# One product of 512 columns instead of two of 256 in the RWKV projections and both output projections of a two-layer trunk

## The chip, the cores and the metric

One NeuronCore of a Trainium2 chip runs the whole program; there is no other core and no collective. The metric is device time of one execution in microseconds (us). The engines are TensorE (PE, matmuls; PEld are its weight loads), VectorE (DVE), ScalarE (ACT), GpSimd (POOL) and SyncE (SP, which issues most transfers). All accumulate or read in float32; the large products are done in the reduced form that the profile shows as fp32r.

## The reference

Two layers over a sequence of 256 tokens of width 2048, each a token mixer and an MLP of width 8192 with a squared ReLU, all modulated by a conditioning vector `c`:

```
mod = c_act @ ada_w[i] + ada_b[i]
hmix = rms_norm(x) * (1 + sc1) + sh1
y = dsa_mixer(hmix, ...)        # layer 0: indexer, top-k, attention, then  out @ w_o
y = rwkv7_mixer(hmix, ...)      # layer 1
x = x + g1 * y
hff = rms_norm(x) * (1 + sc2) + sh2
x = x + g2 * (jnp.square(jax.nn.relu(hff @ mlp_w1[i])) @ mlp_w2[i])
```

Inside the second mixer stand four square products of 2048 by 2048: `r = xr @ w_r`, `k = xk @ w_k`, `v = xv @ w_v`, and at the end `(o * g) @ w_o`. Between them runs a scan over the tokens with a state per head. A last RMS norm closes the program.

## The kernel before, in words

Activations lie transposed: 16 tiles `x[f]` of 128 features by 256 tokens. To keep float32 accuracy with fp32r products, every operand is split into a high part (rounded to fp32r by a cast on ACT) and a low part (the rest, a subtraction on DVE or POOL). A moving tile holds both, side by side, as 128 x 512: columns 0 to 255 high, 256 to 511 low. A weight piece of 128 x 512 becomes two tiles, `whi` (L92) and `wlo` (L94). `acc3` (L178 to L186) multiplies one weight block of 128 x 128 with one moving tile in three matmuls of 256 columns, which all add into the same 256 columns of a PSUM bank: high weights by high part (L184), high weights by low part (L185), low weights by high part (L186). I call these three a term. `dense` takes a bank and runs `acc3` over all terms of one output tile; one call has 16 terms in the projections `b_w_r`, `b_w_k`, `b_w_v`, and 1 to 4 in the output projections.

Who reads the bank: for r, k and v one ACT copy (L735, L863, L899). For an output projection (`out_group`, L402 to L409) one DVE operation, `x[f] = p * gate + x[f]` (L409). The output projection of layer 0 (`a_w_o`) has 48 calls of four terms that run beside the attention heads, and then 16 of three terms and 16 of one term at its end, with L409 reading. The one of layer 1 (`b_w_o`) has 48 calls of four terms and 32 of two terms, of which the last 16 come after the last head of the scan. Counted in terms that is 256 for each of the five: `a_w_o`, r, k, v, `b_w_o`, 1,280 in all.

A PSUM tile takes a whole bank, whatever its width. Kind "d" has two banks, kind "m" two, and "a", "b", "i", "j" one each. `s.kinds` says which kinds `dense` goes through: "d" alone in the heads, for k, for v and in the scan, "dm" for r, and "dcm" at the end of layer 0's output projection and in the MLPs ("c" is "a" and "b" in turn).

The order on each engine is not written out: a scheduler builds it from priorities and its own simulation, and each engine then runs its list strictly in order. So every queue has a fixed order, and a late instruction holds up all behind it. The MLP that follows each mixer begins on DVE, ACT and POOL with its input tiles `h` (L355, L356), which need the finished `x[f]`; each product of the MLP adds over all 16 of them. `ada_block` (L224) puts long products on DVE, in between, for the modulation of later layers.

Of the kernel before, what the change touches and what calls it, by code (L numbers as in the profile page):

```python
# [12 lines left out]
OP = mybir.AluOpType  # L13
# [3 lines left out]
P = 128  # L17
D = 2048
S = 256
# [82 lines left out]
class Trunk:  # L102
# [76 lines left out]
    def acc3(s, out, terms):  # L179
        mm = s.nc.tensor.matmul  # L180
        n = len(terms)
        for i, (wh, wl, m) in enumerate(terms):
            w = m.shape[-1] // 2
            mm(out, wh, m[:, :w], start=i == 0, stop=False)  # L184
            mm(out, wh, m[:, w:], start=False, stop=False)  # L185
            mm(out, wl, m[:, :w], start=False, stop=i == n - 1)  # L186

    def dense(s, w, movs, cols):
        s.turn += 1
# [213 lines left out]
    def out_group(s, name, layer, block, g, movs, first=0):  # L403

        w = s.wload(s.io[name][block * 4 + g, :, first * 512:(first + len(movs)) * 512])
        for o in range(4):
            f = g * 4 + o
            p = s.dense(w, movs, [k * 512 + o * P for k in range(len(movs))])
            s.nc.vector.scalar_tensor_tensor(s.x[f], p, s.m(layer, 2, f), s.x[f], op0=OP.mult, op1=OP.add)  # L409


    def angles(s, freq, which):
# [277 lines left out]
    def rwkv_project(s, keep):  # L690
        nc, io = s.nc, s.io
        mm = nc.tensor.matmul
# [27 lines left out]
        cols = [k * P for k in range(16)]  # L720

        xm = []
        for i in range(NF + LAG):
            if i < NF:
                normed(i)
            if i >= LAG:
                k = i - LAG
# [2 lines left out]
        s.xv = []  # L730
        for f in range(NF):
            w = s.wload(io["b_w_r"][f])
            p = s.dense(w, xm, cols)
            t = s.B()
            nc.scalar.copy(t, p)  # L735
            nc.sync.dma_start(s.rd[f], t)
            wl1 = s.wload(io["b_lora1"][f // 4][:, f % 4 * 448:f % 4 * 448 + 448], "l")
            d = delta(f)
# [2 lines left out]
            for p, m, c in ((hid[0], xw, 0), (hid[1], xa, 96), (hid[2], xg, 192), (hid[3], xg, 320)):  # L741
                wh, wl = wl1.at(c)
# [20 lines left out]
        for f in range(NF + 1):  # L763
            if f < NF:
                w = s.wload(io["b_w_k"][f])
                pk = s.dense(w, xm, cols)
            if f:
                s.elements(f - 1, pp, omka, wa0)
            if f == NF:
                s.vs[0] = s.value(0, keep.tile([P, S], F32, name="v0"))  # L770
            pp = pk
# [52 lines left out]
    def elements(s, f, pk, omka, wa0):  # L824
# [35 lines left out]
        nc.gpsimd.tensor_copy(s.pc[:, f, :].unsqueeze(2), pp[:, :, 64:65])  # L860

        k, kk, sq = s.B(), s.B(), s.B()
        nc.scalar.copy(k, pk)  # L863
        nc.vector.tensor_scalar(kk, k, s.v("k_k", f), None, op0=OP.mult)
        nc.scalar.activation(sq, kk, AF.Square)
        ap = s.B()
# [29 lines left out]

    def value(s, f, v):
        w = s.wload(s.io["b_w_v"][f])
        s.nc.scalar.copy(v, s.dense(w, s.xv, [i * P for i in range(16)]))  # L899
        return v  # L900

    def prepare(s, f):
# [350 lines left out]
```

## Time and profile before

| | |
|---|---|
| median of 3 runs | 2779.71 us (2779.48 to 2797.15) |
| profiled execution | 2790.62 us, span 2788.7 us |
| PE busy | 94% of the span, 24,884 matmuls |
| PE weight loads | 88% |
| DVE busy | 70% |
| ACT, POOL busy | 47%, 48% |
| mean granted TensorE clock | 0.963 of full speed |

The stages, by the first and last instruction of their lines in the trace: layer 0's mixer up to 247 us, its attention heads 247 to 426 us, the end of its output projection from there to about 467 us, overlapping with the first MLP (to 1243 us); r from 1282 to 1390 us, k from 1390 to 1546 us, v and the scan from 1546 to 2010 us, the last output projections to 2040 us, the second MLP to the end. Matmuls are pipelined: the profile gives each a duration of about 0.28 us although the next starts 0.12 us later, so the step from start to start is what a matmul costs, and "busy" is not the same as used to the full. The profiled execution is 0.4% longer than the median of the runs.

### The profile page before, as it was taken

The numbers are of one execution on the slowest core, as the hardware profiler recorded it, in microseconds if no ns is written. First come the engines' busy times: TensorE is split into PE (matmuls) and PEld (weight loads), VectorE is DVE, ScalarE is ACT, GpSimd is POOL, SyncE is SP. The second block draws the span as 40 slices with busy tenths as digits, with TensorE's granted clock in tenths as the row PEclk, the third lists the DMA queues.
The fourth block names the chain that finished last, engine by engine and source line by source line (L and its number), as shares of the span: only waits on it lengthen the run. The fifth ranks groups of instructions, "written<-read, shape, count | busy, mean of one in ns | idle before, by whom it ended". The sixth has DMA issues, their size and how long they took to land. (4 is left out here: it accounts for less than half of the span.)

```text
span 2788.7 us, 64443 instructions
## 1 busy us (share of the span) xinstructions
PE 2630.8 (94%) x24884; PEld 2446.9 (88%) x24884; DVE 1957.3 (70%) x3183; ACT 1309.4 (47%) x2852; POOL 1345.3 (48%) x1121
## 2 busy tenths in 40 slices
PE   6898998999999999988889999999899999999998
PEld 4566778999999999888888888888799999999998
DVE  2266568998999999968787655666688377473553
ACT  3334435445444444446555343444455455454553
POOL 1243327566577576655655411233465445444444
PEclk9899999999999999999999887999999999999999
DMA  9997745889899898855557522343467767555553
GB/s 370 393 339 270 255 135 187 312 308 348 283 338 328 286 347 311 302 167 152 172 181 246 173 83 75 89 117 97 146 225 219 222 213 243 183 182 184 182 183 115
DMA packets 263620, 624.73 MB, mean 224 GB/s; under 512 B 29328, under 2 KB 43024, under 8 KB 238352
## 3 DMA queue, kind: packets, MB, share of 16 engines
q1 hardware_dynamic: 256400, 608.03, 65.2%
q10 hardware_dynamic: 6912, 12.59, 1.2%
q8 instruction: 195, 3.19, 0.5%
q14 instruction: 113, 0.93, 0.1%
HBM read 603.72 MB, written 16.78 MB: 222 GB/s over the span
## 5 line engine op out<-in xcount | busy, mean ns | idle before, releaser
L94 POOL TENSOR_TENSOR wlo<-raw,whi 128x512 fp32r<-128x512 f32 x364 | 587.1, 1622 | 544.5 <-ACT whi L92 417.2
L92 ACT CAST whi<-raw 128x512 fp32r<-128x512 f32 x856 | 513.0, 619 | 404.7 <-PE ps_d L185 149.1
L94 DVE TENSOR_TENSOR wlo<-raw,whi 128x512 fp32r<-128x512 f32 x492 | 436.5, 892 | 222.6 <-ACT whi L92 211.0
L94 POOL TENSOR_TENSOR wlo<-more,whi 128x512 fp32r<-128x512 f32 x181 | 263.7, 1460 | 322.7 <-ACT whi L92 165.6
L224 DVE CUSTOM_DVE_ANT_0 araw<-araw,cb 128x2048 f32<-128x2048 f32 x124 | 342.6, 2776 | 4.6 <-DMA araw<-ada_w_in 4.6
L184 PE MATMUL ps_d<-A,whi 128*128 128x256 f32 x1058 | 309.4, 293 | 10.6 <-ACT B L863 6.2
L92 ACT CAST whi<-more 128x512 fp32r<-128x512 f32 x366 | 222.0, 618 | 199.0 <-PE ps_d L185 48.5
L185 PE MATMUL ps_d<-A,whi 128*128 128x256 f32 x1058 | 303.5, 287 | 2.3 <-DVE A L198 2.2
L186 PE MATMUL ps_d<-A,wlo 128*128 128x256 f32 x1058 | 303.1, 287 | 0.5 <-DVE wlo L94 0.5
L94 DVE TENSOR_TENSOR wlo<-more,whi 128x512 fp32r<-128x512 f32 (+1 forms) x185 | 174.3, 943 | 138.8 <-ACT whi L92 135.6
L184 PEld LDWEIGHTS ps_d<-A,whi 128*128 128x128 f32 x1058 | 205.4, 195 | 26.2 <-ACT B L863 7.2
L185 PEld LDWEIGHTS ps_d<-A,whi 128*128 128x128 f32 x1058 | 205.5, 194 | 4.8 <-DVE A L198 3.8
L186 PEld LDWEIGHTS ps_d<-A,wlo 128*128 128x128 f32 x1058 | 205.5, 194 | 1.5 <-DVE wlo L94 0.7
L375 ACT ACTIVATE B<-B,sm 128x256 f32<-128x256 f32 x128 | 65.3, 510 | 247.5 <-DVE B L374 247.4
L185 PE MATMUL ps_d<-h,whi 128*128 128x258 f32 x552 | 157.5, 285 | 3.7 <-DVE h L356 3.7
L186 PE MATMUL ps_d<-h,wlo 128*128 128x258 f32 x552 | 155.8, 282 | 2.5 <-DVE wlo L94 2.4
L184 PE MATMUL ps_d<-h,whi 128*128 128x258 f32 x552 | 156.7, 284 | 0.0
L184 PE MATMUL ps_m<-h,whi 128*128 128x258 f32 x540 | 153.4, 284 | 0.0
L185 PE MATMUL ps_m<-h,whi 128*128 128x258 f32 x540 | 153.1, 284 | 0.0
L186 PE MATMUL ps_m<-h,wlo 128*128 128x258 f32 x540 | 152.1, 282 | 0.0
L376 DVE TENSOR_TENSOR B<-B 128x256 f32<-128x256 f32 x128 | 111.5, 871 | 52.9 <-ACT B L375 52.9
L184 PE MATMUL ps_m<-A,whi 128*128 128x256 f32 x506 | 145.1, 287 | 1.1 <-ACT whi L92 1.1
(552 smaller groups left out, 8773.8 us busy)
## 6 DMA issues: line engine op xcount, KB each, us to landing
araw<-ada_w_in SPq DMA_DIRECT2D x192, 1024.0 KB, 7.2
raw<-mlp_w_in SPq DMA_DIRECT2D x614, 256.0 KB, 4.6
more<-mlp_w_in SPq DMA_DIRECT2D x410, 256.0 KB, 4.1
raw<-b_w_r_in SPq DMA_DIRECT2D x64, 256.0 KB, 3.6
raw<-b_w_k_in SPq DMA_DIRECT2D x64, 256.0 KB, 3.8
raw<-b_w_v_in SPq DMA_DIRECT2D x64, 256.0 KB, 3.6
raw<-b_w_o_in SPq DMA_DIRECT2D x64, 256.0 KB, 3.5
hd<-A ACTq DMA_DIRECT2D x48, 256.0 KB, 4.3
```

The costliest lines, as they stand in the source:

```text
L92: t.nc.scalar.copy(hi[:, :n], r)
L94: e.tensor_tensor(lo[:, :n], r, hi[:, :n].bitcast(F32), op=OP.subtract)
L184: mm(out, wh, m[:, :w], start=i == 0, stop=False)
L185: mm(out, wh, m[:, w:], start=False, stop=False)
L186: mm(out, wl, m[:, :w], start=False, stop=i == n - 1)
L224: nc.vector.tensor_tensor_reduce(out=w, in0=w, in1=s.cb, scale=1.0, scalar=0.0, op0=OP.mult, op1=OP.add, accum_out=acc[:, k:k + 1])
L375: nc.scalar.activation(r, u, AF.Relu, bias=c)
L376: nc.vector.tensor_tensor(q, r, r, op=OP.mult)
```

## The change

`wide` replaces `dense` in the five places. It gives the whole moving tile (512 columns, high and low) to one matmul with the high weights, so that columns 0 to 255 of the bank collect high by high and columns 256 to 511 high by low; the low weights still meet the high part alone, into columns 0 to 255. A term is then one matmul of 512 columns and one of 256. The two halves of the bank are added afterwards: for r, k and v by `join`, an ACT copy of the right half to a new tile of 256 columns from the ring `B`, then a DVE addition of the left half and that copy; in `out_group` by running the DVE operation twice, once for each half.

```diff
+    def wide(s, w, movs, cols, kind=None):
+        mm = s.nc.tensor.matmul
+        s.turn += 1
+        p = s.bank(kind or s.kinds[s.turn % len(s.kinds)])
+        n = len(movs)
+        for i, (c, m) in enumerate(zip(cols, movs)):
+            wh, wl = w.at(c)
+            if i:
+                mm(p[:, :S], wl, m[:, :S], start=False, stop=False)
+                mm(p, wh, m, start=False, stop=i == n - 1)
+            else:
+                mm(p, wh, m, start=True, stop=False)
+                mm(p[:, :S], wl, m[:, :S], start=False, stop=n == 1)
+        return p
+
+    def join(s, out, p):
+        t = s.B()
+        s.nc.scalar.copy(t, p[:, S:])
+        s.nc.vector.tensor_tensor(out, p[:, :S], t, op=OP.add)
...
-            p = s.dense(w, movs, [k * 512 + o * P for k in range(len(movs))])
-            s.nc.vector.scalar_tensor_tensor(s.x[f], p, s.m(layer, 2, f), s.x[f], op0=OP.mult, op1=OP.add)
+            p = s.wide(w, movs, [k * 512 + o * P for k in range(len(movs))])
+            for k in range(2):
+                s.nc.vector.scalar_tensor_tensor(s.x[f], p[:, k * S:(k + 1) * S], s.m(layer, 2, f), s.x[f],
+                                                 op0=OP.mult, op1=OP.add)
...
-            p = s.dense(w, xm, cols)
+            p = s.wide(w, xm, cols)
             t = s.B()
-            nc.scalar.copy(t, p)
+            s.join(t, p)
...
-                pk = s.dense(w, xm, cols)
+                pk = s.wide(w, xm, cols)
...
-        nc.scalar.copy(k, pk)
+        s.join(k, pk)
...
-        s.nc.scalar.copy(v, s.dense(w, s.xv, [i * P for i in range(16)]))
+        s.join(v, s.wide(w, s.xv, [i * P for i in range(16)]))
```

The scheduler makes a new order of it. Three places, of which the first is on PE, in the last products of r (bank kinds "d" and "m"; `xm` tiles are named `A`, the last four `o`). Before:

```order
L184 MATMUL ps_m<-o,whi 128x256
L185 MATMUL ps_m<-o,whi 128x256
L186 MATMUL ps_m<-o,wlo 128x256
L184 MATMUL ps_m<-o,whi 128x256
L185 MATMUL ps_m<-o,whi 128x256
L186 MATMUL ps_m<-o,wlo 128x256
```

and with the change, where L198 and L199 are the two matmuls of `wide`:

```order
L198 MATMUL ps_d<-A,wlo 128x256
L199 MATMUL ps_d<-A,whi 128x512
L198 MATMUL ps_d<-A,wlo 128x256
L199 MATMUL ps_d<-A,whi 128x512
L198 MATMUL ps_d<-A,wlo 128x256
```

Three rows of a term have become two, one of them 512 wide.

The second is DVE at the seam between layer 0's output projection and the first MLP, where the one-term products are read (L409) and the MLP's first input tiles `h` (L356) are made. Before:

```order
L409 SCALAR_TENSOR_TENSOR x_68<-ps_b,mod_84,x_68 128x256
L409 SCALAR_TENSOR_TENSOR x_69<-ps_m,mod_84,x_69 128x256
L356 SCALAR_TENSOR_TENSOR h<-x_66,mod_84,h 128x256
L409 SCALAR_TENSOR_TENSOR x_70<-ps_d,mod_84,x_70 128x256
L409 SCALAR_TENSOR_TENSOR x_71<-ps_a,mod_84,x_71 128x256
L409 SCALAR_TENSOR_TENSOR x_72<-ps_m,mod_84,x_72 128x256
L94 TENSOR_TENSOR wlo<-raw,whi 128x512
L409 SCALAR_TENSOR_TENSOR x_73<-ps_d,mod_84,x_73 128x256
L356 SCALAR_TENSOR_TENSOR h<-x_67,mod_84,h 128x256
```

and with the change (L409 is now L433, L356 is L379):

```order
L379 SCALAR_TENSOR_TENSOR h<-x_66,mod_84,h 128x256
L433 SCALAR_TENSOR_TENSOR x_72<-ps_m,mod_84,x_72 128x256
L94 TENSOR_TENSOR xlo<-more,xhi 128x512
L433 SCALAR_TENSOR_TENSOR x_73<-ps_d,mod_84,x_73 128x256
L379 SCALAR_TENSOR_TENSOR h<-x_67,mod_84,h 128x256
L433 SCALAR_TENSOR_TENSOR x_70<-ps_d,mod_84,x_70 128x256
L433 SCALAR_TENSOR_TENSOR x_71<-ps_a,mod_84,x_71 128x256
L379 SCALAR_TENSOR_TENSOR h<-x_68,mod_84,h 128x256
L433 SCALAR_TENSOR_TENSOR x_74<-ps_b,mod_84,x_74 128x256
L379 SCALAR_TENSOR_TENSOR h<-x_69,mod_84,h 128x256
L433 SCALAR_TENSOR_TENSOR x_72<-ps_m,mod_84,x_72 128x256
```

Each `x` tile has two readings of a bank now, and the scheduler puts other work between the two. From the last copy of an attention output (L666) to the first result of the MLP (L374) DVE has 39 such readings before and 86 with the change: the 32 calls of the end and seven earlier ones before, the 32 and eleven now. The rest of the list is the same but for one weight piece more.

The third is DVE in k, where before the bank was read by ACT alone and no row of DVE stood for it. With the change (L209 is the addition of `join`, L889 the next use of k, L879 and L918 belong to the same stage):

```order
L879 SCALAR_TENSOR_TENSOR B<-cst,B 128x256
L209 TENSOR_TENSOR B<-ps_d,B 128x256
L889 TENSOR_SCALAR B<-B,vec 128x256
L94 TENSOR_TENSOR llo<-raw,lhi 128x512
L894 TENSOR_SCALAR B<-B,vec,omka 128x256
L895 TENSOR_TENSOR B<-B 128x256
L879 SCALAR_TENSOR_TENSOR B<-cst,B 128x256
L918 SCALAR_TENSOR_TENSOR A<-B,vec 128x256
L94 TENSOR_TENSOR wlo<-raw,whi 128x512
L209 TENSOR_TENSOR B<-ps_d,B 128x256
```

The bank is free for the next product only after that addition, which stands in DVE's list behind work of other kinds.

## Rows read from the trace of the kernel before

**Rows 1.** The page: span, busy time and share of each engine, count.

```profile
span 2788.7 us, 64443 instructions
PE 2630.8 (94%) x24884; PEld 2446.9 (88%) x24884; DVE 1957.3 (70%) x3183; ACT 1309.4 (47%) x2852; POOL 1345.3 (48%) x1121
```

**Rows 2.** Windows of stages: length, busy us of each engine, clock, DMA share.

```profile
core 0: us, PE busy (x) PEld busy (x) DVE busy (x) ACT busy (x) POOL busy (x), PEclk, DMA share, GB/s
...
247.00:426.00 179.00, 166.74 (x1113) 127.02 (x1112) 105.07 (x260) 68.79 (x177) 47.89 (x40) 0.95 0.58 201
...
1282.00:1390.00 108.00, 96.76 (x762) 94.63 (x761) 85.92 (x158) 63.33 (x147) 63.64 (x48) 0.95 0.63 182
1390.00:1546.00 156.00, 141.31 (x1123) 132.96 (x1124) 126.08 (x239) 89.16 (x206) 92.26 (x162) 0.97 0.66 206
...
1617.00:2010.00 393.00, 383.50 (x6673) 329.13 (x6671) 257.27 (x714) 161.76 (x440) 107.11 (x96) 0.94 0.33 95
```

**Rows 3.** Windows of both seams, columns as in rows 2.

```profile
426.00:444.00 18.00, 18.00 (x152) 18.00 (x152) 9.17 (x18) 7.63 (x15) 9.14 (x7) 1.00 0.47 143
444.00:476.00 32.00, 26.65 (x192) 24.85 (x192) 31.66 (x51) 23.74 (x51) 28.96 (x53) 0.95 0.75 252
...
2013.00:2046.00 33.00, 28.07 (x185) 26.84 (x185) 29.21 (x42) 23.47 (x50) 29.06 (x48) 0.82 0.60 190
```

**Rows 4.** Waits of PE from 444 to 492 us: total, times, longest.

```profile
PE ps_d L185 <- DVE h L356: 3.7, 5, 1.6
PE ps_a L185 <- DVE h L356: 2.9, 1, 2.9
```

**Rows 5.** Timeline of PE, 256 columns: start, duration, line, form; 32 steps apart.

```profile
427.15 0.28 PE L184 MATMUL ps_d<-A,whi 128*128 128x256 f32 x1
...
430.99 0.28 PE L186 MATMUL ps_d<-A,wlo 128*128 128x256 f32 x1
```

**Rows 6.** Timeline of PE, 512 columns: 19 steps, then four in another stretch.

```profile
231.59 0.40 PE L591 MATMUL ps_d<-wlo,A 128*128 128x512 f32 x1
...
235.90 0.39 PE L592 MATMUL ps_d<-whi,A 128*128 128x512 f32 x1
...
207.30 0.40 PE L591 MATMUL ps_d<-wlo,A 128*128 128x512 f32 x1
...
208.23 0.40 PE L592 MATMUL ps_d<-whi,A 128*128 128x512 f32 x1
```

**Rows 7.** Groups by line on DVE, heads, scan, and an addition from PSUM.

```profile
L409 DVE SCALAR_TENSOR_TENSOR x<-ps_d,mod,x 128x256 f32<-128x256 f32 x41 | 19.7, 479 | 20.3 <-PE ps_d L186 20.2
...
L94 DVE TENSOR_TENSOR wlo<-raw,whi 128x512 fp32r<-128x512 f32 x63 | 52.7, 841 | 24.6 <-ACT whi L92 21.9 <-PE ps_d L186 1.7 <-PE ps_d L185 0.5
L409 DVE SCALAR_TENSOR_TENSOR x<-ps_d,mod,x 128x256 f32<-128x256 f32 x80 | 38.3, 480 | 20.2 <-PE ps_d L186 19.1
...
L446 DVE TENSOR_TENSOR B<-ps_m,B 128x256 f32<-128x256 f32 x16 | 6.7, 417 | 7.7 <-PE ps_m L444 6.6 <-POOL wlo L94 1.1
```

**Rows 8.** Timeline of DVE at both seams: readings, waits in brackets.

```profile
434.55 0.48 DVE L409 SCALAR_TENSOR_TENSOR x<-ps_d,mod,x 128x256 f32<-128x256 f32 x1 [2.38 <-PE ps_d L186]
...
444.98 0.47 DVE L409 SCALAR_TENSOR_TENSOR x<-ps_m,mod,x 128x256 f32<-128x256 f32 x1
445.37 0.47 DVE L409 SCALAR_TENSOR_TENSOR x<-ps_d,mod,x 128x256 f32<-128x256 f32 x1
...
471.24 4.44 DVE L356 SCALAR_TENSOR_TENSOR h<-x,mod,h 128x256 fp32r<-128x256 f32 x5
...
2046.83 0.16 DVE L266 TENSOR_SCALAR sm<-ps_m 128x2 f32<-128x2 f32 x1 [1.35 <-PE ps_m L306]
```

**Rows 9.** Waits of PE in k, 1390 to 1546 us.

```profile
PE ps_d L184 <- ACT B L863: 6.2, 5, 2.2
```

**Rows 10.** Timeline of PE: a first matmul after a wait, and the next.

```profile
457.25 0.38 PE L184 MATMUL ps_d<-o,whi 128*128 128x256 f32 x1 [0.78 <-DVE x L409]
457.47 0.28 PE L185 MATMUL ps_d<-o,whi 128*128 128x256 f32 x1
```

## Prediction

> **What bounds the kernel now.** I read the page first: PE is busy for 94% of the span, DVE for 70%, ACT and POOL under half [rows 1]. By stages PE is nearly full in all that the change touches: 166.7 of 179 us in the attention heads, 96.8 of 108 in r, 141.3 of 156 in k, 383.5 of 393 in the scan [rows 2]. So PE sets the pace, and time that PE's matmuls give back counts, as long as nobody makes PE wait instead. Two stages differ. At the seam between layer 0's output projection and the first MLP, DVE is busy for 31.66 of 32 us while PE has 26.65 [rows 3], and PE waits there for the tiles `h` that DVE makes, 3.7 and 2.9 us [rows 4]: DVE sets the pace. At the seam after the scan it is 29.21 of 33 us on DVE against 28.07 on PE, at a granted clock of 0.82, a mixture of the two levels [rows 3].
>
> **What the change gives on PE.** It removes 1,280 matmuls of 256 columns, one for each term, and makes 1,280 others twice as wide; the columns streamed stay the same. What it gives is the part of a matmul that doesn't grow with its width. The steps show it. 32 steps of 256 columns take 430.99 - 427.15 = 3.84 us, 0.1200 us each [rows 5]. 19 steps of 512 columns, which layer 0's value projection already has, take 235.90 - 231.59 = 4.31 us, 0.2268 us each [rows 6]. Two narrow ones cost 0.2400 us, one wide one 0.2268: 0.0132 us saved, and 1,280 x 0.0132 = 16.9 us. Another stretch of four wide steps takes 0.93 us, 0.2325 each [rows 6]; by that it would be 0.0075 and 9.6 us. I take 16.9, since the longer stretch has the most steps in a row, and keep 9.6 as the other end.
>
> The Trainium skill speaks against this size: "TensorE: Matmul & The Clock Gate", section "Back-to-back issue gap", has a fixed part of 2.5 ns for each matmul at full clock beside its columns. By that, as an estimate, a term would save 2.5 ns, all of them 3.2 us, and my sum below would come to about +13 us instead of -1. The trace doesn't agree (13.2 ns from its own steps), and the measurement decides.
>
> Of the 16.9 us, the 64 terms at the end of layer 0's projection and the last 32 after the scan stand where DVE sets the pace: 96 x 0.0132 = 1.3 us are not gained. Left: -15.6.
>
> **What it adds, place by place.**
> - *Seam after layer 0.* A reading of a bank with the gate takes 0.479 us [rows 7], and readings back to back start 445.37 - 444.98 = 0.39 us apart [rows 8]; I use 0.40. By the new order DVE has 86 of them in the stretch from the last attention output to the first result of the MLP, where it had 39: 47 x 0.40 = 18.8 us more. Some finds room: DVE is idle for 18.00 - 9.17 = 8.8 us from 426 to 444 us, where it waits for PE (2.38 us in one row) [rows 3, 8], and for 0.3 us after that. Left are 18.8 - 9.1 = 9.7 us. Four of the 43 calls stood ahead of the stretch before, so that their first readings (1.6 us) only moved into it. I take +8. The bounds: 0, if PE's own remaining products cover it, and 12.8 (the 32 calls of the end, without any idle time used). What is late next is `h`: its 16 operations stand at the end of this list [rows 8], and the MLP cannot finish one product without the last of them.
> - *Seam after the scan.* 16 second readings, 16 x 0.40 = 6.4 us. DVE is idle for 33.00 - 29.21 = 3.8 us in that stretch [rows 3], of which 1.35 us lie behind the last `h` [rows 8]. 6.4 - 2.5 = 3.9; I take +4, between 0 and 6.4.
> - *k.* Before, PE waited five times, 6.2 us in all, for the ACT copy that frees a bank of kind "d" [rows 9]. Now the DVE addition comes after the copy: an operation that reads PSUM and a tile takes 0.417 us [rows 7], and it stands in DVE's list behind work of other kinds, one weight piece of 0.84 us at most by its mean [rows 7]. Five times 0.42 to 1.26 is 2.1 to 6.3 us; I take +3. DVE, busy for 126 of 156 us there [rows 2], has room for 16 x 0.42 = 6.7 us.
> - *r and v.* 32 additions of 0.42 us. r goes through four banks and a product fills one in 16 x (0.2268 + 0.1200) = 5.5 us, so a bank is needed again 16 us later; in v, 5.5 us and the scan's own work lie between. Cost 0; without that cover, 0.42 each, 13 us.
> - *48 calls beside the heads, 64 in the scan.* A call of four terms fills a bank in 4 x 0.347 = 1.39 us while the other bank is read, twice, in 0.88 us. The margin is 0.5 us. In the heads DVE stood idle for 20.3 us ahead of its 41 readings and waited for PE, 0.5 us each; in the scan 20.2 us ahead of 80, 0.25 each [rows 7]. DVE is mostly there before the product ends, so I cost the second reading at 0. Its price without cover is the second rival.
> - *Order and rings.* `join` takes one more `B` tile for each output tile. The new order keeps r, k, v and the scan's steps in the same sequence, with output calls of the scan a little earlier than before. SP's transfers are the same ones; no queue gets a new kind of wait but PE, where 150 first matmuls now also wait for PE's own earlier product in that bank, which the reading that frees the bank needed anyway: 0. Within the first MLP the order is shuffled; I have no price for that but a few us of either sign.
>
> Sum: -16.9 + 1.3 + 8 + 4 + 3 = -0.6 us. Against the profiled execution that is 2790.6 - 0.6 = 2790.0 us, and against the median of the runs, which is 0.4% lower, 2779.1. I say 2779 us: **no change that can be told**. A measurement of this kernel tells about 1% from no change (28 us).
>
> **The rivals.**
> - *A: PE's own work covers the seams.* DVE's extra readings are spread over the end of layer 0's projection, where PE still has products to do, and the gain stays: 2779.7 - 16.9 = 2763 us (2756 to 2771). For it: PE's waits for `h` were only 6.6 us in that stretch [rows 4], so PE had other work. Against it: DVE's 31.66 of 32 us [rows 3] leave no place for readings that all stand ahead of the last `h`.
> - *B: the second reading holds the bank, and PE waits.* In the heads and the scan each call has two readings and two banks. The point from which it decides is the margin of 0.5 us: where a reading finds DVE in a weight piece of 0.84 us [rows 7], PE's next call starts late by 0.3 us or more, and a first matmul after a wait takes 457.47 - 457.25 = 0.22 us instead of 0.12 [rows 10]. If half of the 48 + 64 calls lose 0.4 + 0.1 us, that is 56 x 0.5 = 28 us, and with the sum above 2779 + 28 = 2807 us; with a quarter of them 2793, with all 2835. For it: DVE goes from 257 of 393 us in the scan to 257 + 64 x 0.40 + 13 x 0.42 = 288, 73% [rows 2]. Against it: the idle time ahead of the readings [rows 7].
> - *C: the wide matmul saves less than its steps show*, because its pace falls to 0.2325 us or below that gain in the busier stages [rows 6]: with 9.6 us saved instead of 16.9, 2779 + 7 = 2786 us. (By the rule of the Trainium skill's page above it would be some 2793 us.)
>
> **How the numbers follow.** The forecast (2771 to 2788 us) gets 0.50, A 0.20, B 0.20, C 0.06, and 0.04 is left for a new order that helps or harms by more than all this. Within B half lies below 2807.5 us, which is 1% above the median. Slower by over 1%: half of B and a little of the rest, 0.11. Faster by over 1% (below 2752 us) needs more than all that PE's steps can give, so only the order could do it: 0.04. Within 1%: 0.85. For 8 in 10 the range takes the forecast and A down to 2760 us, C, and B up to about its middle: 2760 to 2804 us.
>
> **What would show it.** Right: steps of 0.227 us for the 512-column matmuls and 0.120 for the narrow ones; the stretch from the last attention output to the first MLP result longer by about 8 us with DVE without gaps, and the second seam by about 4; r and v shorter by 3.4 us each (256 x 0.0132); PE's waits in k on DVE instead of ACT, some 3 us longer. Wrong: waits of PE on the second L409 in the heads or the scan adding up to over 10 us (B), a first seam of the same length (A), wide steps over 0.23 us (C). A change in a stage that has none of the new matmuls, the first MLP above all, would mean that the new order did it and not the product.

## The result: 0.9% slower, and the profile after

The median of the changed kernel is 2808.51 us (7 runs, 2802.92 to 2813.77) against 2779.48 us for the kernel before in the same comparison (2771.6 to 2797.15): ratio 1.0086, 95% interval 1.0066 to 1.0107, so about 24 us slower by the ratio (the two medians lie 29 us apart). Forecast was 2779 us and a range of 2760 to 2804: the time lies outside it.

The page of the changed kernel, to be read against [rows 1]:

```profile
span 2805.1 us, 62263 instructions
PE 2626.7 (94%) x23604; PEld 2369.6 (84%) x23604; DVE 1997.3 (71%) x3391; ACT 1308.4 (47%) x2852; POOL 1335.8 (48%) x1121
```

PE has 1,280 matmuls fewer and is busy for 4 us less; DVE has 208 operations and 40 us more. The span is 16.4 us longer. The windows of the stages (columns as in [rows 2]; heads, first seam, first MLP, r, k, prefix and scan of the heads with v, second seam):

```profile
247.00:424.00 177.00, 158.98 (x913) 112.28 (x912) 116.23 (x289) 65.98 (x173) 47.55 (x38) 0.94 0.55 198
424.00:501.00 77.00, 65.32 (x362) 54.68 (x361) 71.39 (x132) 39.38 (x78) 48.73 (x66) 0.87 0.56 187
501.00:1259.00 758.00, 733.68 (x6011) 731.05 (x6010) 671.41 (x722) 354.77 (x721) 455.75 (x261) 0.99 0.86 302
...
1300.00:1403.00 103.00, 93.14 (x561) 82.19 (x559) 86.50 (x170) 59.59 (x139) 63.76 (x47) 0.96 0.59 185
1403.00:1562.00 159.00, 141.93 (x869) 121.75 (x868) 132.85 (x253) 88.30 (x207) 96.09 (x160) 0.93 0.64 202
...
1590.00:2019.00 429.00, 413.15 (x6945) 327.72 (x6946) 297.15 (x851) 174.70 (x473) 110.20 (x100) 0.93 0.30 95
2019.00:2068.00 49.00, 38.54 (x209) 32.56 (x210) 36.87 (x64) 28.10 (x58) 34.53 (x59) 0.83 0.58 195
```

The second row shows the loss best: the first seam is 77 us long where it was 66, DVE has 71 of them, PE 65. To compare kernels whose instructions are moved about, I cut each trace at the same events (first head, last output of the first MLP, first and last of the small side products with `b_lora1` that run beside r, first preparation of the scan, last output tile of the scan, first result of the second MLP). "Layer 0 block" is heads, first seam and first MLP together, so that work which only crosses the seam doesn't count. Lengths in us:

| stretch | before | before, again | changed | changed, again | change in the first pair | forecast |
|---|---|---|---|---|---|---|
| layer 0 block | 995.9 | 995.4 | 1012.0 | 1011.8 | +16.2 | +5.5 |
| of it: first seam | 66.3 | 66.3 | 76.5 | 76.5 | +10.2 | |
| of it: first MLP | 750.8 | 750.5 | 757.9 | 757.9 | +7.1 | |
| start of layer 1 | 39.3 | 39.0 | 41.5 | 41.5 | +2.2 | 0 |
| r | 107.3 | 107.3 | 102.5 | 102.9 | -4.8 | -3.4 |
| k, to the scan's start | 183.4 | 184.7 | 187.4 | 189.1 | +4.0 | -0.4 |
| scan with v | 437.1 | 430.3 | 429.2 | 427.1 | -7.9 | -6.3 |
| second seam | 41.6 | 42.3 | 48.7 | 48.9 | +7.1 | +4.0 |

The forecast column is the prediction's own sum spread over the stretches (13.2 ns for each of 256 terms in r, k, v, and so on). In the first pair the start and the second MLP differ by 0.2 us or less. The first products of r already run in "start of layer 1", so that row and r belong together. By the ratio the kernels lie 24 us apart, and the two profiled executions 16; the scan, which is the stretch that differs most between two executions of one kernel, comes back to this below.

How the wide products run, on PE's timeline in r (start, duration, line, form); seven pairs lie between these rows:

```profile
1345.53 0.28 PE L198 MATMUL ps_m<-A,wlo 128*128 128x256 f32 x1
1345.64 0.39 PE L199 MATMUL ps_m<-A,whi 128*128 128x512 f32 x1
...
1347.99 0.28 PE L198 MATMUL ps_m<-o,wlo 128*128 128x256 f32 x1
```

2.46 us for seven pairs is 0.3514 us a term. Three narrow steps took 3 x 0.1200 = 0.3600 [rows 5]. A term saves 8.6 ns and not 13.2, all 1,280 some 11.0 us and not 16.9. The Trainium skill ("TensorE: Matmul & The Clock Gate", section "Back-to-back issue gap") has a fixed part of 2.5 ns for each matmul at full clock, which as an estimate would be saved once a term; the trace's 8.6 ns lies between that and my figure.

PE's waits in the changed kernel (waiting tile and line, what it waited for: us in all, times, longest), first in the heads, then in the first seam, in k and in the second seam:

```profile
PE ps_d L201 <- DVE x L433: 2.9, 4, 1.5
...
PE ps_b L201 <- DVE x L433: 4.9, 4, 2.7
PE ps_d L201 <- DVE x L433: 3.2, 4, 1.7
PE ps_m L201 <- DVE x L433: 2.8, 4, 1.1
...
PE ps_d L201 <- DVE B L209: 10.0, 4, 4.5
PE ps_d L199 <- DVE A L221: 2.9, 5, 2.2
...
PE ps_d L201 <- DVE x L433: 5.5, 7, 1.7
```

In the first seam PE waited for `h` before (6.6 us, [rows 4]); now it waits 10.9 us for banks that DVE has still to read. In k the wait on ACT's copy (6.2 us, [rows 9]) has become one of 10.0 us on DVE's addition. That names the last link only. The chain that ended the longest of these waits:

```profile
1535.43 0.62 ACT L92 CAST lhi<-raw 128x512 fp32r<-128x512 f32 x1 [3.68 <-DMA raw<-b_lora_in]
...
1537.00 0.35 ACT L208 COPY B<-ps_d 128x256 f32<-128x256 f32 x1
...
1537.38 0.42 DVE L209 TENSOR_TENSOR B<-ps_d,B 128x256 f32<-128x256 f32 x1 [0.61 <-ACT B L208]
...
1537.86 0.80 PE L201 MATMUL ps_d<-A,whi 128*128 128x512 f32 x1 [4.49 <-DVE B L209]
```

DVE stood idle before the addition; ACT's copy was late, behind a cast that waited 3.68 us for a piece of the side weights `b_lora2` to land. ACT's waits for these pieces add up to 22.2 us in k, where they were 12.6 before:

```profile
ACT lhi L92 <- DMA raw<-b_lora_in: 22.2, 12, 3.7
```

```profile
ACT lhi L92 <- DMA raw<-b_lora_in: 12.6, 13, 2.5
```

DVE's groups, with the two readings, in the heads and in the first seam (count | busy, mean ns | idle before):

```profile
L433 DVE SCALAR_TENSOR_TENSOR x<-ps_d,mod,x 128x256 f32<-128x256 f32 x73 | 34.7, 479 | 14.7 <-PE ps_d L199 13.7
...
L433 DVE SCALAR_TENSOR_TENSOR x<-ps_d,mod,x 128x256 f32<-128x256 f32 x43 | 20.2, 477 | 2.5 <-PE ps_d L199 2.0
L379 DVE SCALAR_TENSOR_TENSOR h<-x,mod,h 128x256 fp32r<-128x256 f32 x16 | 11.4, 726 | 0.0
L433 DVE SCALAR_TENSOR_TENSOR x<-ps_m,mod,x 128x256 f32<-128x256 f32 x22 | 10.0, 471 | 0.0
L433 DVE SCALAR_TENSOR_TENSOR x<-ps_b,mod,x 128x256 f32<-128x256 f32 x12 | 5.7, 472 | 0.5 <-PE ps_b L199 0.5
L433 DVE SCALAR_TENSOR_TENSOR x<-ps_a,mod,x 128x256 f32<-128x256 f32 x10 | 4.7, 470 | 0.0
```

Each reading costs what it cost before, 479 ns [rows 7], and there are twice as many. In the seam (the last five rows) DVE comes to `h` without any idle time. In the middle of this seam PE is granted 1.2 GHz (0.50 in the row) and is busy for 11.59 of 17.10 us, while DVE has no gap:

```profile
469.00:486.10 17.10, 11.59 (x38) 8.86 (x39) 17.10 (x37) 11.14 (x27) 11.27 (x13) 0.50 0.37 132
```

### The profile page after: what moved, and what is told of

The parts are those of the page before. It is cut to its first block, busy times and chain, and to the rows that moved or that the text cites. A ratio compares the mean times of both kernels' runs of the same rounds, so it can differ in the third digit from the quotient of the medians.

```text
span 2805.1 us, 62263 instructions
## 1 busy us (share of the span) xinstructions
PE 2626.7 (94%) x23604; PEld 2369.6 (84%) x23604; DVE 1997.3 (71%) x3391; ACT 1308.4 (47%) x2852; POOL 1335.8 (48%) x1121
## 5 line engine op out<-in xcount | busy, mean ns | idle before, releaser
L94 POOL TENSOR_TENSOR wlo<-raw,whi 128x512 fp32r<-128x512 f32 x364 | 562.4, 1553 | 650.6 <-ACT whi L92 563.7
L94 DVE TENSOR_TENSOR wlo<-raw,whi 128x512 fp32r<-128x512 f32 x492 | 429.0, 877 | 217.7 <-ACT whi L92 208.9
L184 PE MATMUL ps_d<-A,whi 128*128 128x256 f32 x578 | 168.7, 292 | 0.5 <-ACT A L634 0.3
L185 PE MATMUL ps_d<-A,whi 128*128 128x256 f32 x578 | 164.8, 285 | 2.7 <-DVE A L402 2.7
L186 PE MATMUL ps_d<-A,wlo 128*128 128x256 f32 x578 | 164.4, 285 | 0.0
L199 PE MATMUL ps_d<-A,whi 128*128 128x512 f32 x408 | 156.2, 416 | 3.0 <-DVE A L221 2.9
L433 DVE SCALAR_TENSOR_TENSOR x<-ps_d,mod,x 128x256 f32<-128x256 f32 x276 | 129.5, 478 | 31.0 <-PE ps_d L199 26.7
L198 PE MATMUL ps_d<-A,wlo 128*128 128x256 f32 x408 | 118.7, 294 | 0.0
L184 PEld LDWEIGHTS ps_d<-A,whi 128*128 128x128 f32 x578 | 111.5, 193 | 7.5 <-issue 2.8
```

Source lines behind the costliest of these rows:

```text
L94: e.tensor_tensor(lo[:, :n], r, hi[:, :n].bitcast(F32), op=OP.subtract)
L198: mm(p[:, :S], wl, m[:, :S], start=False, stop=False)
L199: mm(p, wh, m, start=False, stop=i == n - 1)
L433: s.nc.vector.scalar_tensor_tensor(s.x[f], p[:, k * S:(k + 1) * S], s.m(layer, 2, f), s.x[f], op0=OP.mult, op1=OP.add)
```

## The experiments

Theory 1 at the start: the second readings make the loss, at the seams above all. Ratios are to the kernel before, measured beside it on the same chip.

**The kernel before, again.** 

> The program before, unchanged, for a second profiled execution. The first one (2790.6 us) lay 11 us above the median of its runs (2779.5), the one of the change (2806.9) 2 us below its own. Theory 1 (the extra 11 us of the first profile lie in one stage): this profile is nearer to 2780 us, and one or two stages are 5 to 11 us shorter than in the first, so that the first MLP, which came out 7 us longer with the change, is some 5 to 15 us longer against this one. Rival (spread all over): every stage is shorter by 0.2 to 0.6% and no stage stands out.

Its span was 2786.7 us; the stretches are in the table above. All but two agree within 1.3 us; the start takes 3 us more and the scan 6.8 us less. So the first profile of the kernel before wasn't odd, and differences of a few us in the scan or at the start say nothing by themselves.

**r, k and v only.** The output projections stay as before.

```diff
-            p = s.wide(w, movs, [k * 512 + o * P for k in range(len(movs))])
-            for k in range(2):
...
+            if False:
+                p = s.wide(w, movs, cols)
...
+            else:
+                p = s.dense(w, movs, cols)
+                s.nc.vector.scalar_tensor_tensor(s.x[f], p, s.m(layer, 2, f), s.x[f], op0=OP.mult, op1=OP.add)
```

> The wide product and the addition in r, k and v alone; both output projections as before. Theory 1 (the loss is the second reading on DVE at the two seams, the rest gains): faster than before by 3 to 9 us (r about -4, k -1 to +3, v and the scan -2 to -5, both seams 0), 2771 to 2777 us. Rival (the addition behind ACT and DVE holds the banks of k and v, and that is where the 24 us go): slower than before by 5 us or more. A third (any new order of the scheduler costs): slower by 5 us or more with the time in the first MLP, which has none of the new matmuls.

Measured: 2794.49 us, ratio 1.0026 (1.0011 to 1.0040). The gain that theory 1 forecast for this part isn't there. r is 4.2 us shorter, but k up to the scan's start takes 191.8 us, 8.4 more, so the joins are no small matter; by the number it is the rival that came true.

**The output projection of layer 0 only** (`if layer == 0`: wide and two readings, else as before).

> The wide product in layer 0's output projection alone, with two readings; r, k, v and layer 1's output as before. Theory 1: the seam to the first MLP is longer by about 10 us, the heads shorter by 1 to 2, and the sum slower than before by 8 to 20 us, the first MLP being the open part (0 to +12). Rival (r, k, v hold the loss): within 3 us of before.

Measured: 2789.24 us, ratio 1.0011 (0.9994 to 1.0027). By the total, some 3 us, the rival holds; by the stretches theory 1 does: the layer 0 block takes 1004.4 us, 8.5 more than before, the first seam 76.1. Yet r, whose code is that of before, is 4.5 us shorter, and the scan takes 418.2 us, 12 to 19 less than in the two executions of before. The lists of PE and DVE are in another order there: a part that wasn't touched can move by more than the part that was.

This run shows one thing more. By source line and tile name the lists of all five engines in its layer 0 block are those of the changed kernel, and yet that block took 1012.0 and 1011.8 us there (and 1009.5 in the kernel "k with ACT freeing the bank" below, whose lists there are the same too). Of the 7.6 us to 1012.0, 6.8 are time at the half clock, counted as length times one minus the granted clock (23.9 us against 30.7). In the same way the six executions whose DVE list in this block is the one of before, but for at most one added copy (before, again, one more tiny operation, and the three in which layer 0 is untouched) take 990.4 to 998.2 us. A difference of a few us in the block is therefore not put down to its instructions.

**The output projection of layer 1 only** (`if layer == 1`).

> The wide product in layer 1's output projection alone, with two readings. Theory 1: the seam to the second MLP longer by about 7 us, the scan ahead of it shorter by 3 to 5; sum +1 to +5 us, 2780 to 2785 us; the first MLP is the same to 2 us, since nothing ahead of it changes. Rival (the second readings hold banks inside the scan): slower by 10 us or more, with PE waiting for the readings within the scan.

Measured: 2792.51 us, ratio 1.0023 (1.0003 to 1.0043). Second seam 45.9 us, 4.3 more. By the ratio that is some 6 us, just above theory 1's range; the scan's 432.7 us lie between the two executions of before, so the 3 to 5 us that it was to gain aren't seen.

**One more tiny operation.** What is a new order worth alone?

```diff
+            if layer == 0 and block == 0 and f == 0:
+                s.nc.vector.tensor_copy(s.x[f][:, :1], s.x[f][:, :1])
```

> The kernel before with one more DVE operation: a copy of one column of one x tile onto itself at the first call of layer 0's output projection. By itself it costs about 0.1 us of DVE; but the scheduler makes another order of it nearly everywhere. Theory 1 (a new order alone is worth a few us of either sign in a stage and up to 10 us in k and the scan): stages differ from the kernel before by 2 to 10 us here and there, total within 0.4% of it. Rival (the order is worth nothing, what moved in the changed kernel and in the partial ones came from their own instructions): every stage within 1.5 us, ratio 1.000 within 0.1%.

Measured: 2785.94 us, ratio 1.0004 (0.9985 to 1.0023). The stretches stay: 990.8, 39.1, 106.3, 185.3, 436.9 and 42.5 us; the layer 0 block moved by 5 us (all of it time at the half clock, 15.4 us where the kernel before has 20.5), the others by 2 at most. But the expectation's premise was wrong: by line and tile name the executed lists of PE and DVE in the heads, r, k and the scan are those of before to 99.7% and more; what I had taken for a new order there was new buffer numbers. So this run is a third execution of the old order (its scan takes 436.9 us where the other two take 437.1 and 430.3) and decides nothing on what a new one is worth. The run with layer 0's projection alone does: there the scan's lists agree with before to less than a third by the same comparison.

**Dense seams.** The 32 calls at the end of layer 0's projection and the 16 behind the scan as before, all else as in the changed kernel.

```diff
+            if not (block == 3 and (layer == 0 or first == 2)):
+                p = s.wide(w, movs, cols)
...
+            else:
+                p = s.dense(w, movs, cols)
```

> The changed kernel, but the 32 calls at the end of layer 0's output projection and the 16 calls after the last head of the scan are as before (three matmuls of 256 columns a term, one DVE reading). Theory 1 (the seams are lost to the second DVE readings): seam 1, from the last attention copy to the first MLP result, goes back from 76.5 to about 66 us, seam 2 from 48.7 to about 42; together 15 to 17 us less than the changed kernel, so about 2790 to 2794 us on this chip's scale where the kernel before is 2787, ratio to before 1.000 to 1.003. Rival (the seams are long because the new order or the clock puts other work there): seam 1 stays over 72 us, ratio to before 1.006 to 1.010. Neither theory lets it beat the kernel before by more than 0.3%.

Measured: 2807.37 us, ratio 1.0090 (1.0068 to 1.0112), no better than the changed kernel. Theory 1 in this form falls. The second seam is back (42.8 us), the first only by half (71.1), and the layer 0 block at 1004.5 us is still 8.6 over the kernel before. What the seams gave back is lost in k (190.5), in the scan (434.1) and at the start (3 us).

**Wide products first, narrow ones after them.**

```diff
         for i, (c, m) in enumerate(zip(cols, movs)):
-            wh, wl = w.at(c)
...
+            mm(p, w.at(c)[0], m, start=i == 0, stop=False)
+        for i, (c, m) in enumerate(zip(cols, movs)):
+            mm(p[:, :S], w.at(c)[1], m[:, :S], start=False, stop=i == n - 1)
```

> The changed kernel, but within one call all 512-column products come first and all 256-column ones after them, where they alternate in the changed kernel. Theory 1 (it is the alternation of widths that makes a wide and a narrow step cost 0.353 us together, instead of 0.227 + 0.120 = 0.347): the calls of 16 terms in r, k and v show wide steps of 0.227 and narrow ones of 0.118, some 0.006 us a term less, 5 us over the 768 terms of r, k and v, and 2 to 3 us more in the 512 others: ratio to the kernel before about 1.006 where the changed kernel has 1.009. Rival (a wide step costs 0.233 us or more wherever it stands, the saving is 7 ns a term at best): steps in r, k and v stay at 0.350 to 0.355 us a pair, same time as the changed kernel within what a new order does.

Measured: 2844.32 us, ratio 1.0214 (1.0193 to 1.0235). In r the median steps are 0.232 (wide) and 0.120 us, together 0.352; alternating they are 0.234 and 0.118, also 0.352. The alternation costs nothing; the wide matmul itself takes about 0.232 in such streams, as the shorter of the two stretches in [rows 6] had it. The kernel is slower for another reason, for the most part, which the row of its scan shows:

```profile
1592.00:2047.00 455.00, 429.05 (x6930) 342.95 (x6931) 303.16 (x842) 172.24 (x472) 109.96 (x99) 0.89 0.28 90
```

455 us at a granted clock of 0.89, where the changed kernel has 429 at 0.93.

**k with ACT freeing the bank.**

```diff
-        s.join(k, pk)
+        k2 = s.B()
+        nc.scalar.copy(k, pk[:, :S])
+        nc.scalar.copy(k2, pk[:, S:])
+        nc.vector.tensor_tensor(k, k, k2, op=OP.add)
```

> The changed kernel, but in k two ACT copies take both halves out of the bank and the DVE addition reads those two tiles, so that ACT frees the bank as before. Theory 1 (in k the bank is held by the DVE addition, some 3 to 7 us): PE's waits for bank d in k, 10.0 us behind the DVE addition in the changed kernel, go down to 5 to 8 us and stand on ACT; the stage of k is 2 to 5 us shorter than the changed kernel's 158.6, ratio to the kernel before 1.007 to 1.008. Rival (k is not held by the join, its length follows from the order): the waits move to ACT with the same sum, the stage keeps 158 us within 2.

Measured: 2814.12 us, ratio 1.0111 (1.0092 to 1.0130). The wait went where theory 1 put it:

```profile
PE ps_d L201 <- ACT B L890: 4.8, 6, 1.3
```

and k up to the scan's start is 1.9 us shorter (185.5), but the scan is 11.5 us longer (440.7, at a clock of 0.90), which neither theory had.

**One reading everywhere, and one in the output projections alone.** Both read only the left half of a bank in the output projections (the upper edit); the first also has one copy in place of the join (the lower edit).

```diff
-            for k in range(2):
+            for k in range(1):
...
-        t = s.B()
-        s.nc.scalar.copy(t, p[:, S:])
-        s.nc.vector.tensor_tensor(out, p[:, :S], t, op=OP.add)
+        s.nc.scalar.copy(out, p[:, :S])
```

> The changed kernel with the wide products everywhere, but only the left half of each bank is read: one DVE operation a call in the output projections, one ACT copy in r, k and v. It leaves out the products of the high weights with the low part of the moving tile, which are computed and never read. Theory 1 (the loss of the changed kernel is the second readings, and the wide products by themselves save some 8.5 ns a term, 10.9 us in all): seams of 66 and 42 us as before, k not longer than 156 us, total 8 to 14 us below the kernel before, ratio 0.995 to 0.997. Rival (the wide products themselves, or what a new order does with them, make the loss): ratio 1.002 or more, with the lost time in the heads and the scan.

> The changed kernel with the joins of r, k and v kept, but in the two output projections only the left half of the bank is read, so that the products of the high weights with the low part are left out there. Theory 1: the seams and the heads as in the kernel before, k longer by 3 to 7 us for the join; total between the run with one reading everywhere and the kernel before, ratio 0.998 to 1.001. Rival (the join costs nothing, all of the loss is in the output projections): the same time as with one reading everywhere within 3 us.

Measured: 2779.45 us, ratio 0.9979 (0.9964 to 0.9994), and with the joins kept 2789.78 us, 1.0009 (0.9993 to 1.0025). The layer 0 block takes 991.9 and 993.1 us, 3 to 4 less than before, the second seam 41.5 and 40.5, as before or less. The joins make k up to the scan's start 6.8 us longer (182.3 and 189.1); the waits in k, with one copy and with the join:

```profile
PE ps_d L201 <- ACT B L207: 5.2, 4, 2.7
```

```profile
PE ps_d L201 <- DVE B L209: 11.0, 4, 4.7
```

So the loss comes with the readings and joins, not with the wide products; by what way, is taken up below. And even without any second reading the gain is only some 6 us in the medians, less than the 8 to 14 expected.

**The kernel before, every bank of the output projections read twice.**

```diff
+            z.scalar_tensor_tensor(s.x[f], p, s.m(layer, 2, f), s.x[f], op0=OP.mult, op1=OP.add)
+            z.scalar_tensor_tensor(s.x[f], p, 0.0, s.x[f], op0=OP.mult, op1=OP.add)
```

> The kernel before, products as they were (three matmuls of 256 columns a term), but in the two output projections DVE reads every bank twice: the second time it adds zero times the bank. Theory 1 (the second readings are the loss): seam 1 longer by 8 to 11 us, seam 2 by 4 to 7, the heads by 3 to 5; total ratio 1.006 to 1.009. Rival (second readings are hidden outside the seams and the wide products or the order make the rest): seams as said, but total ratio no more than 1.004. If the seams keep 66 and 42 us, theory 1 falls.

Measured: 2792.49 us, ratio 1.0024 (1.0005 to 1.0043). Its first seam and its scan, then its waits in the first seam:

```profile
419.00:495.00 76.00, 66.20 (x451) 61.42 (x450) 68.77 (x132) 38.18 (x77) 48.98 (x66) 0.84 0.58 187
...
1583.00:2001.00 418.00, 407.92 (x7366) 350.92 (x7367) 293.08 (x831) 172.11 (x472) 109.46 (x99) 0.96 0.33 98
```

```profile
PE ps_d L184 <- DVE x L411: 2.7, 5, 1.3
PE ps_b L184 <- DVE x L411: 2.0, 1, 2.0
PE ps_m L184 <- DVE x L411: 1.9, 2, 1.7
PE ps_a L184 <- DVE x L411: 1.7, 1, 1.7
```

Without a single wide product the first seam is 75.5 us long, the layer 0 block 11.0 us over the kernel before, the second seam 6.4 us over. That is theory 1 for the seams; the heads, which it had 3 to 5 us longer, are 4.4 us shorter (174.3), and the total is only 0.24% up, as the rival said, since the scan takes 418 us: with 59 more readings in it than before it is the shortest of all. So second readings cost nothing there that shows. In the layer 0 block the time at the half clock goes from 20.5 to 32.4 us, as much as the block is longer.

**Dense seams and dense k, twice profiled.** The run with dense seams, and k with `dense` and one ACT copy.

> The run with dense seams, and k too as in the kernel before (three matmuls, one ACT copy); wide products remain in r, v, 48 calls of the heads and 64 of the scan. Theory 1 (the join in k holds a bank and costs 3 to 7 us more than its products save): k at 156 to 158 us with PE's waits on ACT, ratio to the kernel before 1.003 to 1.007 where the run with dense seams has 1.009. Rival (k's length is the order's doing): k between 149 and 163 us with no relation to the join, ratio 1.007 to 1.011.

Measured: 2812.38 us, ratio 1.0092 (1.0070 to 1.0115). k up to the scan's start is 181.5 us, 5.9 less than in the changed kernel (183.9 in its second execution, 5.2 less than in the changed kernel's), and both parts of theory 1 hold by their stretches; the time does not move, because the scan takes 452.5 us. Is that the kernel or this execution?

> The run with dense seams and dense k, a second profiled execution. If the half clock in its scan belongs to the kernel, the scan again takes about 452 us with 52 us lost to it; if it belongs to the execution, it falls to between 418 and 445 us with the difference at 401 us within 2.

> The changed kernel, a second profiled execution. If the half-clock time of the scan belongs to the kernel, the scan takes 429 us within 3 again, with 28 us lost to the half clock (length times one minus the granted clock); if it belongs to the execution, both move together by 5 us or more and their difference stays at 401 us within 2. The seams should stay at 76.5 and 48.7 us within 1.5.

The scans of the first and of the second execution of this kernel, in two fences:

```profile
1578.00:2031.00 453.00, 432.44 (x6950) 343.72 (x6950) 305.14 (x852) 173.60 (x474) 113.03 (x100) 0.88 0.29 92
```

```profile
1580.00:2028.00 448.00, 426.44 (x6950) 338.57 (x6950) 306.55 (x852) 173.84 (x474) 113.41 (x100) 0.90 0.29 93
```

and of the changed kernel's second execution:

```profile
1593.00:2020.00 427.00, 411.72 (x6946) 326.22 (x6946) 297.64 (x851) 174.87 (x473) 110.50 (x100) 0.94 0.31 96
```

So it is both: about 2 to 7 us differ between executions, and some 20 us between the two kernels come back each time. Multiply length by clock: 453 x 0.88 = 399, 448 x 0.90 = 403, 427 x 0.94 = 401, 429 x 0.93 = 399, and in the fences above 455 x 0.89 = 405 and 418 x 0.96 = 401. (The kernel before has 437 us at 0.92, that is 402.) At the full clock the scan is about 400 us in these kernels, with one reading or two, with wide products or narrow (by the unrounded clock 399 to 404 in sixteen of the eighteen profiled executions; 396 where ACT frees k's bank, 408 with r, k and v only). What differs is how long PE is granted 1.2 GHz instead of 2.4.

**r only.** Wide products and the join in r, all else as before.

> The kernel before with the wide product and its join in r alone (256 terms, four banks, ACT and DVE with room). Theory (the wide product saves 7 to 10 ns a term and r has cover for the join): r 4 to 5 us shorter, the other stages as before but for the order and the clock, ratio 0.996 to 1.000. Rival (the join disturbs DVE's list and the gain is lost before k ends): r 2 us shorter or less, or k longer by as much, ratio 1.000 to 1.004.

Measured: 2781.42 us, ratio 0.9983 (0.9965 to 1.0000). r takes 102.5 us, 4.8 less, for 256 terms; k up to the scan's start 3.7 more although nothing in k was touched, the scan 426.0:

```profile
1573.00:1999.00 426.00, 410.45 (x7382) 353.68 (x7382) 280.84 (x773) 174.48 (x474) 113.01 (x100) 0.95 0.33 101
```

The only complete version that isn't slower than the kernel before; a gain of 0.2% at best, which the interval doesn't separate from none.

**Four products at the end of layer 0's projection.** There the low weights too meet all 512 columns, which adds the product of low weights and low part.

```diff
+                if four:
+                    mm(p, wl, m, start=False, stop=False)
+                else:
+                    mm(p[:, :S], wl, m[:, :S], start=False, stop=False)
...
+                       four=layer == 0 and block == 3)
```

> The changed kernel, but in the 32 calls at the end of layer 0's output projection (64 terms) the low weights too meet the whole moving tile, 512 columns: 64 x 0.116 = 7.4 us more work for PE in seam 1, readings as in the changed kernel. Theory (DVE's readings set the pace there and PE has that time to spare): seam 1 stays at 76 to 79 us, total as the changed kernel within 0.2%. Rival 1 (PE sets the pace): seam 1 at 82 to 85 us, total 7 us more. Rival 2 (the seam is long because PE ran at half clock after its waits): with more to do PE keeps the full clock and seam 1 falls below 74 us.

Measured: 2809.89 us, ratio 1.0091 (1.0066 to 1.0115). The first seam is 81.5 us, near rival 1, but the first MLP 746.3, so that the layer 0 block with 7.4 us more work takes 1005.3 us, 6.7 less than in the changed kernel. The added work doesn't show over the whole block. But 5.1 of the 6.7 us are less time at the half clock (25.6 us against 30.7), and executions with equal lists differ by as much, so this run doesn't settle which engine sets the block's length. Rival 2 falls by its sign, the seam, which is longer and not below 74 us.

## Why the prediction was wrong, step by step

- **"48 calls beside the heads ... I cost the second reading at 0": this step failed, and it is the largest.** With dense ends, where the second readings stand in the four-term calls alone, the layer 0 block is 1004.5 us (1004.0 and 1004.3 with dense k too); with one reading it is 993.1 and 991.9, and in the six executions with the old block 990.4 to 998.2. That is 11.4 us for 48 readings by the pair with the joins kept, and 6 at the least. The half clock doesn't make it: at length times clock the three blocks with dense ends are 979 to 980 us, the others 971 to 976. PE doesn't wait on banks for it (2.9 us in the heads, 2.1 in the scan), so it isn't rival B. The second readings made DVE's list longer: before the last attention copy DVE reads 37 calls (74 readings) instead of 41 [rows 7], the rest slides behind it, and with dense ends 54 readings stand in the first seam where 39 did. The first MLP too is mostly longer in the kernels with two readings (753.4 to 757.9 us, but 746.3 with four products) than in those with one (747.9 and 748.4); old blocks have 747.1 to 753.0, and which waits make it isn't settled. By the prediction's own sign a longer first MLP means that the new order did it; the kernels with one reading, also in a new order, don't have it. Nor is 11.4 us for 48 a price: with the old products all 80 readings made the block 11.0 us longer.
- **"Seam after layer 0 ... +8": near by size, not shown as a price.** From dense ends to the changed kernel the block grows by 1012.0 - 1004.5 = 7.5 us, with DVE without gaps as forecast, though PE waits for banks now and not for `h`. But the kernel with layer 0's projection alone, which has the changed kernel's lists there, takes 1004.4 us, no more than dense ends, so the agreement is in part luck. The seam by itself grows from 71.1 to 76.5.
- **"16.9" for the wide product: too large.** 8.6 ns a term and 11.0 us in all; the other end that I kept, 9.6 us, was nearer. I took the longer stretch of steps in [rows 6] because it was longer; the alternating and the grouped stream both run at the shorter one's pace. Rival C was right in its mechanism.
- **"k ... +3": too small, and the wait was another.** The join costs 6.8 us by the pair of runs with and without it, over the bound of 6.3; each is one execution, and two of one kernel differ by 1.3 and 1.7 us here. The step was that the addition comes late by the work ahead of it in DVE's list, one weight piece at most. In all four waits DVE stood idle before the addition, 0.6 to 1.1 us, until ACT's copy came. In the two longest (2.9 and 4.5 us) that copy stood behind a cast that waited 2.90 and 3.68 us for a piece of `b_lora2`. From the start of k to the scan ACT waits 21.6 to 24.8 us for such pieces in the six executions with wide k, join and alternating products, 9.1 with the grouped ones, and 11.1 to 17.4 in those without the join or with ACT freeing the bank. So "SP's transfers are the same ones ... 0" fell short too: they land later against ACT's list. Why they do isn't shown.
- **"Seam after the scan ... +4": too small in the changed kernel.** 48.7 us against 42.8 with a dense end and 40.5 with one reading: 6 to 8 us, at or over the bound of 6.4. The idle time that I subtracted didn't take the readings. Other kernels with two readings there have 45.9 to 50.1, so +4 isn't excluded for them.
- **r: right in size**, 4.8 and 4.4 us shorter instead of 3.4; with the start of layer 1, where its first products run, 2.6 and 1.9. But r was also 4.5 us shorter where its products were the old ones and only the order was new, so how much of it is the product's isn't settled.
- **The scan's readings at 0: right**, by the 418 us of the kernel with every bank read twice (401 at length times clock). But the gain of 6.3 us in v and the scan isn't visible: at the full clock the scan takes 400 us, as before.
- **What was left out: the granted clock.** [Rows 3] had 0.82 at the second seam and I called it a mixture of the two levels, but no term of the sum or of the range came from it. In the scan alone length times one minus the clock runs from 17 us (418 x 0.04) to 54 us (453 x 0.12), more than any term of the sum. In the scan of the first pair this helped the changed kernel: by the unrounded clock its scan loses 28.2 us to the half clock and that of before 35.9, which is 7.7 of the 7.9 us by which it is shorter. Elsewhere it went the other way: 30.7 us against 20.5 in the layer 0 block, 13.5 against 6.4 in k, and over the whole execution 118.5 against 102.1, as much as the 16.4 us between the two. The second pair has 115.2 against 106.4, with 19.3 us between them. The mean clock of every run is on record, also of those without a profile: 0.957 to 0.962 in the seven of the changed kernel, 0.956 to 0.972 in 92 of the kernel before. By it 115 us stand against 101 in the mean, so some 14 of the 22 us between these means are time at the half clock, and 8 are left. Which is cause and which effect isn't shown. The changed seam at 469.0 to 486.1 us, with DVE full and PE waiting, is a stretch where the low clock need not cost anything; in the scan, where length times clock stays the same, it does.

The new order got 0.04 of the chance and no term. It is worth more than that: untouched code in another order gave a scan 12 to 19 us shorter (layer 0's projection alone), and the two versions with dense seams and with dense k have scans 5 and 23 us longer than the changed kernel, each time through the granted clock. Even the same lists moved the layer 0 block by 7.6 us. I could have had it in the range as an unknown of either sign, since the prediction says itself that a new order is made of everything.

## What to carry to other kernels

Merging matmuls saves only the fixed part of a step, here 8.6 ns a term, and pays with readings on another engine, here 0.4 to 0.5 us a call: price the readings first, over the whole stretch up to the next point where everything must be finished, and not only where the engine is full already. An operation put between a product and the release of its bank is late by all that it waits for: in the first seam by what stands ahead of it in DVE's list, in k by another engine's copy and the transfer behind that. A wait that is put down to an operation is followed back one link further before that operation is blamed. And where a stage shows a granted clock below one, hold length times clock beside length before a difference there is put down to instructions.

## What the runs showed of the hardware

Over granted clocks from 0.88 to 0.96, length times clock of the scan stays within 2% of 401 us in kernels with quite different lists. PE was busy for 94% to 98% of these scans by the records, and still was granted 1.2 GHz for a part of them. What in a kernel's order decides how long it stays there wasn't found. A matmul of 512 columns takes 0.232 to 0.234 us in r by the median, whether its neighbours are wide or narrow.
